# HGRN2 scores of both directions issued together, the last head pair's products moved, weight splits held back

## The chip, the cores and the metric

The kernel runs on one core of a Trainium2 chip. The metric is the device time of one execution in microseconds, median of several. TensorE (PE in the profile) multiplies, VectorE (DVE), ScalarE (ACT) and GpSimd (POOL) work on vectors, SyncE (SP) issues most transfers.

## The reference

Two transformer blocks over 256 tokens of width 1024, all in float32. The first has an HGRN2 mixer over a context of 256 tokens and the 256 latent tokens, in two directions, and a convolutional feed-forward part. The second has retention, sliding-window attention and a second feed-forward part. The change touches the mixer alone:

```python
b = jnp.cumsum(logf, axis=3)
qe = q * jnp.exp(b - b_ref)
ke = k * jnp.exp(b_ref - b)
scores = jnp.where(mask, jnp.einsum('bhnik,bhnjk->bhnij', qe, ke), 0.0)
o_intra = jnp.einsum('bhnij,bhnjv->bhniv', scores, v)
kv = jnp.einsum('bhnjk,bhnjv->bhnkv', k * jnp.exp(b_last - b), v)
...
o_inter = jnp.einsum('bhnik,bhnkv->bhniv', q * jnp.exp(b), s_start)
o = (o_intra + o_inter).reshape(Bn, H, T, v.shape[-1])
...
return (rmsnorm(o, g_gain) * jax.nn.silu(g)) @ w_out
```

There are 8 heads of width 128, chunks of 64 tokens, and for the second direction everything is flipped in time. Only the latent tokens are read out.

## The kernel before

Weights come from HBM in pieces of 512 KB (a half of a chunk) into eight buffers `raw`. Each piece is split in two float32r tiles: `hi` is its rounded copy (ACT, L155), `lo` the rest (DVE, L156). The activations `hT` are split likewise, and a product is three matmuls, weight hi by x hi, hi by lo and lo by hi (`mm3`, L352 to L354). The splits of pieces to come are recorded wherever a chunk is taken or given back (`use`, `part_done`, `release`, all through `pump`), as far ahead as there are free split buffers (five in `split`; more pools come and go). Each engine runs its instructions in the order in which the program records them.

The heads go in four pairs, p = 0 to 3. For each pair there are the products of both forget gates (ff, fb), of q and of v; then gate work on DVE and ACT (`gates`, one generator for each direction d, run step by step together). The attention itself is small float32 work that PE does between the large products. It is queued in `side` and taken out by `tick`, four ticks in a product. For a head hh of the pair it is:

- `T_`: transposes of the decayed context keys `kc`, copied out by ACT to `kcT`
- `SC_`: scores of a direction. 32-column pieces of `ke` against `qe` (L647, L649), the 128x128 block between the two halves of the tokens (L652), and the 64x64 blocks between chunks (L658). They are written to one PSUM bank, masked and copied out by DVE (`copy_predicated`, L664) and ACT; for the second direction DVE adds both into `scm` (L669)
- `S_`: the state from the context (`kcT` by v), `O_`: the output, its squares (ACT) and its norm (POOL and DVE) into `on`
- `OT_`: transposes of `on`, copied to `oTs`

A float32 matmul stands as two passes in the profile, a float32r one as one. For p = 0 to 2 this side work is taken during the next pair's products. For p = 3 it is taken during the four products of g (`C["g", 0..3]`, called G0 to G3 here), by the table `slots`. After each of these, `oTs` of a pair is multiplied by the silu of g (L891) and split into `yh`, `yl` (`split_y`). Then comes the output product `o1` (`row_product`): `go(0)` for the first of its four chunks, and `finish` for the other three, which runs token half 0 first, then `o1_done` on it (DVE L1016 and L1017, ACT), then token half 1, the transposes of the normed rows to `hT` (L978) and the first feed-forward products (L342). `ada_flush` puts the sums of a modulation vector through two matmuls by ones (L599) and adds them (L600).

Of the kernel before, what the change touches and what calls it, by code (L numbers as in the profile page):

```python
# [18 lines left out]
T = 256  # L19
# [32 lines left out]
def kernel(ctx: ExitStack, tc: tile.TileContext, a, out):  # L52
# [42 lines left out]
                   kind)  # L95

    loaded, ready = {}, {}
    at_ = {"l": 0, "s": 0, "u": 0, "rel": 0}
    raw_seq, split_pools = [], []

    class SplitPool:
# [14 lines left out]
    def pump(limit, hold=False):  # L116

        while True:
            go_on = False
            while at_["l"] < len(halves):  # L120
                i = at_["l"]
                parts, k, n, kind = halves[i]
                if kind != "own":
                    o = raw_seq[-RAW_BUFS] if len(raw_seq) >= RAW_BUFS else -1
                    if o >= 0 and not (o < at_["s"] if halves[o][3] == "split" else o < at_["rel"]):
                        break
                    raw_seq.append(i)
                    r = raws.tile([128, 1024], F32, tag="raw", name="raw")
                    rv = r[:, :k * n].rearrange("p (k c) -> p k c", k=k)
                    loaded[i] = (r, rv)  # L130
                else:
                    rv = None
                for f, src in parts:
                    nc.sync.dma_start(f(rv), src)
                at_["l"] += 1
                go_on = True
            i = at_["s"]
            if i < min(len(halves), limit) and i < at_["l"]:
                _, k, n, kind = halves[i]
# [24 lines left out]
            if not go_on:  # L164
                return
# [371 lines left out]
    xr = []  # L537
    for i in range(2):
        t = res.tile([128, D], F32, name=f"x{i}")
        nc.scalar.dma_start(t, a["x"][0][i * 128:(i + 1) * 128, :])  # L540
        xr.append(t)


    yk = hgy.enter_context(tc.tile_pool(name="hgy", bufs=2))
# [72 lines left out]
    def hg_side(p, el, vt):  # L617
# [17 lines left out]
            St[hh] = wk.tile([128, 2, 128], F32, tag="St", name="St")  # L635
            s_.activation(flat(St[hh]), z[:, 0:256], AF.Copy)

        def SC_(hh, d):
            e = el[d]
            z = bank("x")  # L640
            zd = z[:, 0:256].rearrange("p (b t) -> p b t", b=2)
            ha, hb = (0, 32) if d == 0 else (32, 0)
            for b in range(2):
                for c in range(2):
                    o = hh * 256 + b * 128 + 64 * c
                    ra, rb = slice(64 * c + ha, 64 * c + ha + 32), slice(64 * c + hb, 64 * c + hb + 32)
                    t_.matmul(zd[ra, b, 64 * c:64 * c + 64], e["ke"][:, o + ha:o + ha + 32], e["qe"][:, o:o + 64],  # L647
                              start=True, stop=True)
                    t_.matmul(zd[rb, b, rb], e["ke"][:, o + hb:o + hb + 32], e["qe"][:, o + hb:o + hb + 32],  # L649
                              start=True, stop=True)  # L650
            b1, b2 = e["blk"]
            t_.matmul(z[:, 256:384], flat(e["K"][:, hh, b1, e["k"], :]), flat(e["Q"][:, hh, b2, e["c"], :]),  # L652
                      start=True, stop=True)
            rA = slice(0, 64) if d == 0 else slice(64, 128)
            cB = slice(64, 128) if d == 0 else slice(0, 64)
            zo = z[:, 384:512].rearrange("p (b t) -> p b t", b=2)
            for b in range(2):
                t_.matmul(zo[rA, b, :], e["K"][:, hh, b, e["sA"], :], e["Q"][:, hh, b, e["sB"], :],  # L658
                          start=True, stop=True)
            sc = sc_t[d, hh]  # L660
            for c in range(2):
                for r, q_ in ((slice(64 * c, 64 * c + 64), hb), (slice(64 * c + ha, 64 * c + ha + 32), ha)):
                    i = slice(64 * c + q_, 64 * c + q_ + 32)
                    v_.copy_predicated(sc[r, :, i], hmask[r, d:d + 1, i].to_broadcast([r.stop - r.start, 2, 32]),  # L664
                                       zd[r, :, i])
            s_.activation(sc[rA, :, cB], zo[rA], AF.Copy)
            if True and d:
                scm[hh] = wk.tile([128, 2, 128], F32, tag="scm", name="scm", bufs=2)
                v_.tensor_add(scm[hh], sc_t[0, hh], sc)  # L669
            xS[hh, d] = wk.tile([128, 128], F32, tag="xs", name="xs", bufs=4)  # L670
            s_.activation(xS[hh, d], z[:, 256:384], AF.Copy)

        def O_(hh):
            z = bank("x")
            hc = slice(hh * 128, (hh + 1) * 128)
            for b in range(2):
                terms = []
                for d in range(2):
                    e = el[d]
                    b1, b2 = e["blk"]  # L680
                    ql = flat(e["Q"][:, hh, b, e["c"], :]) if b == b1 else e["q2"][:, hh, :]
                    terms.append((ql, St[hh][:, d, :]))
                    if hh in scm:
                        if d:
                            terms.append((scm[hh][:, b, :], vt[:, 2 + b, hc]))
                    else:
                        terms.append((sc_t[d, hh][:, b, :], vt[:, 2 + b, hc]))
                    if b == b2:
                        terms.append((xS[hh, d], vt[:, 2 + b1, hc]))
                for i, (l, r) in enumerate(terms):  # L690
                    t_.matmul(z[:, b * 128:(b + 1) * 128], l, r, start=i == 0, stop=i == len(terms) - 1)  # L691
            ss = small.tile([128, 2], F32, tag="ss2", name="ss2")
            on[hh] = wk.tile([128, 256], F32, tag="on", name="on")
            for b in range(2):
                c = slice(b * 128, (b + 1) * 128)
                s_.activation(on[hh][:, c], z[:, c], AF.Square, accum_out=ss[:, b:b + 1])
# [5 lines left out]
        def OT_(hh):  # L702
            z = bank("x")
            for b in range(2):
                t_.transpose(z[:, b * 128:(b + 1) * 128], on[hh][:, b * 128:(b + 1) * 128], ident)
            s_.activation(oT[p][:, hh, :], z[:, 0:256], AF.Identity, scale=vec("gn"))

        order = [(T_, 0), (T_, 1), (SC_, 0, 0), (SC_, 0, 1), (SC_, 1, 0), (SC_, 1, 1), (S_, 0), (S_, 1),
                 (O_, 0), (O_, 1)]
        late = [(OT_, 0), (OT_, 1)]  # L710
        return tuple([lambda f=f: f[0](*f[1:]) for f in x] for x in (order, late))

# [1 line left out]
    for p in range(4):  # L714
# [59 lines left out]
        def gates(d):  # L774
# [14 lines left out]
            s_.activation(kcv, kcv, AF.Exp)  # L789
            yield  # L790
            v_.tensor_mul(kcv, kcv, kt_[:, 0])

            b = wk.tile([128, 512], F32, tag="b", name="b")
            for hh in range(2):
# [48 lines left out]
            q2 = wk.tile([128, 2, 128], F32, tag="q2", name="q2")  # L843
            for hh in range(2):
                v_.tensor_scalar(q2[:, hh, :], flat(Q[:, hh, b2, cq, :]), EE[:, hh:hh + 1], None, op0=OP.mult)
            el[d] = dict(kc=kcv, qe=qe, ke=ke, Q=Q, K=K, q2=q2, sA=sA, sB=sB, c=cq, k=ck, blk=(b1, b2))
        wv = use(C["v", p])
        gen = [gates(0), gates(1)]
        live = [True, True]
# [1 line left out]
        while any(live):  # L851
# [4 lines left out]
            if nstep in v_steps[p]:  # L856
# [2 lines left out]
                tick(1)  # L859
                if half:  # L860
                    release(C["v", p])
        work, late = hg_side(p, el, vt)
        if p < 3:
            side.extend(work)


    T0, T1, SC00, SC01, SC10, SC11, S0, S1, O0, O1 = work
    OT0, OT1 = late
    slots = [[], [[T0], [T1], [], [SC00]], [[S0], [SC10, S1], [SC01], [SC11]], [[O0], [O1], [], [OT0]]]
    ys = {}  # L870

    def split_y(p):
# [7 lines left out]
    for p in range(4):  # L880
        for x in slots[p]:
            side.append(lambda x=x: [f() for f in x])
        z = fm_product(C["g", p], x=lambda k: hT(k, 256, 512), tag="m", ticks=1)
        drain()
        if p == 2:
            ada_flush()
        if p == 3:
            OT1()
        sg = wk.tile([128, 512], F32, tag="q", name="sg", bufs=2)
        s_.activation(sg, z, AF.Silu)  # L890
        v_.tensor_mul(oTs[:, p, :], oTs[:, p, :], sg)  # L891
        if p:
            split_y(p - 1)
    split_y(3)
    hg.close()
    o1x = ctx.enter_context(ExitStack())
    SplitPool(o1x, "o1split", 6, chunks[C["ug", 1]][1])
# [3 lines left out]
    def row_product(name, n, lhs, done):  # L901
# [7 lines left out]
            mm3(acc[2 * tok + half], lhs(j, kk, tok), (w[kk][0][:, c], w[kk][1][:, c]),  # L909
                j == 0 and kk == 0, j == n - 1 and kk == 1)  # L910

        def go(j):
            if not acc:
                acc.extend(bank("m") for _ in range(4))
            w = use(C[name, j])
            for kk in range(2):
                for tok in range(2):
                    for half in range(2):
                        mms(j, w, kk, tok, half)
                if kk == 0:  # L920
                    part_done(C[name, j])

# [101 lines left out]

    hTh, hTl = h_at(0)
    go, finish = row_product("o1", 4, act_lhs(ys), o1_done)
    for p in range(4 - SKEW):
        go(p)
    f1 = finish(chunks[C["uv", 0]][1])
    nc.scalar.dma_start(vr[:, 1, :], row_bcast(a["b_ada"], 5 * D, D))  # L1030
    gb[5] = vr[:, 1, :]
# [476 lines left out]
```

## Time and profile before

| | |
|---|---|
| median of 3 runs | 875.5 us (874.65 to 876.54) |
| the profiled execution's own time | 873.8 us |
| its span, first to last instruction | 872.0 us |
| PE busy | 856.8 us, 98% of the span |
| PE weight loads | 778.4 us, 89% |
| DVE busy | 599.5 us, 69% |
| ACT busy | 497.8 us, 57% |
| mean granted TensorE clock | 0.997 |

A busy share is an average over the whole span. What limits a stage is seen in that stage, from the rows in order of time and what ended each wait. In the rows below, a matmul's duration includes the fill and the drain of the array, so durations of neighbours overlap; a price on PE is the distance from one start to the next.

### The profile page before, as it was taken

The page shows a single profiled execution, that of the slowest core. Times are in us where ns is not written, and L with a number is a line of the kernel's source. Part 1 is how long each engine was busy: PE and PEld are TensorE (multiplying, and loading weights), DVE is VectorE, ACT ScalarE, POOL GpSimd, SP SyncE. Part 2 cuts the span into 40 slices and gives each one's busy share as a digit, 9 for nine tenths or more (in the row PEclk, how much of TensorE's full clock was granted, in tenths as well). Part 3 has the DMA queues.
Part 4 walks back from the last instruction along what each step waited for, and adds up shares of the span by engine and source line. Part 5 has one row for each costly group of instructions (what it writes and reads, how often), then busy time and mean ns, then how long its engine had stood idle before and what let it go on. Part 6 is the DMA issues. An engine that isn't in the chain of part 4 may idle for free.

```text
span 872.0 us, 15429 instructions
## 1 busy us (share of the span) xinstructions
PE 856.8 (98%) x6216; PEld 778.4 (89%) x6216; DVE 599.5 (69%) x935; ACT 497.8 (57%) x807; POOL 16.3 (2%) x27
## 2 busy tenths in 40 slices
PE   8999999999999999999999999999999999999997
PEld 7688898989978999999998799999999899999995
DVE  5577969776888688977768646765485687555532
ACT  4587474855856666555555646666553675444421
POOL 0000000000000000000000000000000100000000
PEclk9999999999999999999999999999999999999999
DMA  9893653825437368776753574545696097566401
GB/s 355 277 337 109 184 180 125 287 73 170 144 123 240 122 214 272 265 240 203 259 179 85 157 218 119 147 144 165 196 309 201 6 317 247 184 190 190 148 1 49
DMA packets 116360, 161.99 MB, mean 186 GB/s; under 512 B 13888, under 2 KB 95808, under 8 KB 116288
## 3 DMA queue, kind: packets, MB, share of 16 engines
q1 hardware_dynamic: 113984, 155.80, 55.4%
q10 hardware_dynamic: 2304, 5.20, 1.8%
q8 instruction: 49, 0.80, 0.4%
q14 instruction: 23, 0.19, 0.1%
HBM read 159.93 MB, written 1.05 MB: 185 GB/s over the span
## 4 chain that ended last, share of the span: by engine, by line
PE 89%; DVE 5%; ACT 3%; DMA 1%; issue 1%; POOL 0%; SPq 0%; POOLq 0%; DVEq 0%; ACTq 0%
PE m L352 17%; PE m L353 17%; PE m L354 17%; PE x L352 8%; PE x L353 8%; PE x L354 8%; PE x L691 1%; DVE lo L156 1%; PE m L342 1%; PE x L342 1%; PE m L343 1%; PE m L338 1%; PE x L343 1%; PE x L338 1%; DMA raw<-in_f0w_dram 1%
## 5 line engine op out<-in xcount | busy, mean ns | idle before, releaser
L156 DVE TENSOR_TENSOR lo<-raw,hi 128x1024 fp32r<-128x1024 f32 (+1 forms) x248 | 291.1, 1204 | 128.4 <-ACT hi L155 124.5
L155 ACT ACTIVATE hi<-raw 128x1024 fp32r<-128x1024 f32 (+1 forms) x248 | 249.6, 1039 | 115.9 <-PE x L353 47.7
L352 PE MATMUL m<-hT,hi 128*128 128x256 f32 (+1 forms) x560 | 178.2, 318 | 1.4 <-ACT hT L428 1.4
L353 PE MATMUL m<-hT,hi 128*128 128x256 f32 (+1 forms) x560 | 170.5, 304 | 0.5 <-DVE hT L435 0.5
L354 PE MATMUL m<-hT,lo 128*128 128x256 f32 (+1 forms) x560 | 170.8, 305 | 0.1
L352 PE MATMUL x<-hT,hi 128*128 128x256 f32 x592 | 166.5, 281 | 0.0
L353 PE MATMUL x<-hT,hi 128*128 128x256 f32 x592 | 165.9, 280 | 0.0
L354 PE MATMUL x<-hT,lo 128*128 128x256 f32 x592 | 165.9, 280 | 0.0
L352 PEld LDWEIGHTS m<-hT,hi 128*128 128x128 f32 x560 | 105.6, 189 | 12.2 <-issue 5.1
L354 PEld LDWEIGHTS x<-hT,lo 128*128 128x128 f32 x592 | 113.0, 191 | 0.0
L352 PEld LDWEIGHTS x<-hT,hi 128*128 128x128 f32 x592 | 111.4, 188 | 1.0 <-ACT hi L155 0.2
L353 PEld LDWEIGHTS x<-hT,hi 128*128 128x128 f32 x592 | 111.1, 188 | 1.0 <-issue 0.2
L353 PEld LDWEIGHTS m<-hT,hi 128*128 128x128 f32 x560 | 105.7, 189 | 5.9 <-DVE hT L435 1.1
L354 PEld LDWEIGHTS m<-hT,lo 128*128 128x128 f32 x560 | 105.4, 188 | 5.8 <-DVE lo L156 0.3
L352 PE MATMUL m<-hi,ah 128*128 128x512 f32 x248 | 96.7, 390 | 0.0
L354 PE MATMUL m<-hi,al 128*128 128x512 f32 x248 | 96.6, 390 | 0.0
L353 PE MATMUL m<-lo,ah 128*128 128x512 f32 x248 | 96.6, 389 | 0.0
L354 PEld LDWEIGHTS m<-hi,al 128*128 128x128 f32 x248 | 46.6, 188 | 9.8 <-DVE al L1149 0.2
L353 PEld LDWEIGHTS m<-lo,ah 128*128 128x128 f32 x248 | 46.6, 188 | 8.8
L352 PEld LDWEIGHTS m<-hi,ah 128*128 128x128 f32 x248 | 46.5, 188 | 8.7
L582 DVE SCALAR_TENSOR_TENSOR vr<-raw,cs,vr 128x1024 f32<-128x1024 f32 x28 | 35.9, 1281 | 0.4
L352 PE MATMUL m<-hi,hT 128*128 128x256 f32 x128 | 35.8, 280 | 0.0
(302 smaller groups left out, 1250.7 us busy)
## 6 DMA issues: line engine op xcount, KB each, us to landing
raw<-in_ffn_w_up_dram SPq DMA_DIRECT2D x44, 512.0 KB, 5.6
raw<-in_w_in_dram SPq DMA_DIRECT2D x42, 512.0 KB, 4.1
raw<-in_hg_w_in_dram SPq DMA_DIRECT2D x36, 512.0 KB, 5.0
raw<-in_w_ada_dram SPq DMA_DIRECT2D x32, 512.0 KB, 5.0
raw<-in_w_up_dram SPq DMA_DIRECT2D x32, 512.0 KB, 4.7
raw<-in_w_down_dram SPq DMA_DIRECT2D x32, 512.0 KB, 3.7
raw<-in_ffn_w_down_dram SPq DMA_DIRECT2D x22, 512.0 KB, 4.3
raw<-in_ada_dram SPq DMA_DIRECT2D x16, 512.0 KB, 6.2
```

What stands on the lines that cost most here:

```text
L155: s_.activation(h[:, :w], r[:, :w], AF.Copy)
L156: held.append(lambda r=r, h=h, l=l, w=w: v_.tensor_tensor(l[:, :w], r[:, :w], h[:, :w].bitcast(F32), op=OP.subtract))
L338: t_.matmul(o, hTl[:, k, c], w[k][0], start=False, stop=k == KT - 1)
L342: t_.matmul(o, hTh[:, k, c], w[k][0], start=k == 0, stop=False)
L343: t_.matmul(o, hTh[:, k, c], w[k][1], start=False, stop=False)
L352: t_.matmul(o, wh, xh, start=start, stop=False)
L353: t_.matmul(o, wh, xl, start=False, stop=False)
L354: t_.matmul(o, wl, xh, start=False, stop=stop)
L582: v_.scalar_tensor_tensor(acc, w[kk][0], cs[:, k:k + 1], acc, op0=OP.mult, op1=OP.add)
L691: t_.matmul(z[:, b * 128:(b + 1) * 128], l, r, start=i == 0, stop=i == len(terms) - 1)
```

## The change

1. `SC_` now does both directions of a head in one call: first the two 128x128 matmuls, then all 32-column matmuls of both directions, dealt round the four groups of 32 output partitions. The 64x64 blocks are cut into two 32-column matmuls each. The masks and copies of both directions follow. A place in the queue that it frees is filled with a call that does nothing.
2. For p = 3, G0 is recorded inside the gate loop, right behind the second half of v, with `T_` of both heads in its last two ticks. `S_` goes into G1, the first scores to the end of G2, the second scores and `O_` into G3, `OT_` into `go(0)` of the output product.
3. The table `at_["cap"]` holds back the splits of weights: none of `o1` before the second scores, one piece more at `go(0)`, the rest behind the last `split_y`. `ada_flush` moves there too.
4. The last pair's `on` and its silu of g live in the second half of `x`, whose load moves from the start of the mixer to behind these splits (on the ACT queue).

```diff
-            if i < min(len(halves), limit) and i < at_["l"]:
+            if i < min(len(halves), limit, at_["cap"]) and i < at_["l"]:
...
-        nc.scalar.dma_start(t, a["x"][0][i * 128:(i + 1) * 128, :])
+    nc.scalar.dma_start(xr[0], a["x"][0][0:128, :])
...
-        def SC_(hh, d):
+        def SC_(hh):
...
+            zs, groups = [], [[] for _ in range(4)]
+            for d in range(2):
+                e = el[d]
+                z = bank("x")
+                zs.append(z)
+                b1, b2 = e["blk"]
+                t_.matmul(z[:, 256:384], flat(e["K"][:, hh, b1, e["k"], :]), flat(e["Q"][:, hh, b2, e["c"], :]),
+                          start=True, stop=True)
...
+                for b in range(2):
+                    for i in range(2):
+                        g = 2 * d + i
+                        groups[g].append((zo[32 * g:32 * g + 32, b, :], e["K"][:, hh, b, e["sA"], 32 * i:32 * i + 32],
+                                          e["Q"][:, hh, b, e["sB"], :]))
+                    for c in range(2):
+                        o = hh * 256 + b * 128 + 64 * c
+                        ga, gb_ = 2 * c + ha // 32, 2 * c + hb // 32
+                        rb = slice(32 * gb_, 32 * gb_ + 32)
+                        groups[ga].append((zd[32 * ga:32 * ga + 32, b, 64 * c:64 * c + 64],
+                                           e["ke"][:, o + ha:o + ha + 32], e["qe"][:, o:o + 64]))
+                        groups[gb_].append((zd[rb, b, rb], e["ke"][:, o + hb:o + hb + 32],
+                                            e["qe"][:, o + hb:o + hb + 32]))
+            for n in range(max(len(g) for g in groups)):
+                for g in groups:
+                    if n < len(g):
+                        t_.matmul(*g[n], start=True, stop=True)
...
-        order = [(T_, 0), (T_, 1), (SC_, 0, 0), (SC_, 0, 1), (SC_, 1, 0), (SC_, 1, 1), (S_, 0), (S_, 1),
-                 (O_, 0), (O_, 1)]
+        order = [(T_, 0), (T_, 1), (SC_, 0), (len, ()), (SC_, 1), (len, ()), (S_, 0), (S_, 1), (O_, 0), (O_, 1)]
...
+                    if p == 3:
+
+                        side.extend([lambda: None] * 2 + work[0:2])
+                        zg = fm_product(C["g", 0], x=lambda k: hT(k, 256, 512), tag="m", ticks=1)
...
-    slots = [[], [[T0], [T1], [], [SC00]], [[S0], [SC10, S1], [SC01], [SC11]], [[O0], [O1], [], [OT0]]]
+    slots = [[], [[S0], [S1], [], []], [[], [], [], [SC0]],
+             [[SC1, lambda: splits_to(o1_at[0] + 1)], [], [O0], [O1]]]
...
-    for p in range(4 - SKEW):
-        go(p)
+    at_["cap"] = o1_at[1]
+    side.extend([lambda: None, OT0, lambda: None, OT1])
+    go(0, 1)
+    drain()
+    v_.tensor_mul(oTs[:, 3, :], oTs[:, 3, :], sg)
+    split_y(3)
+    ada_flush()
+    splits_to(1 << 30)
+    nc.scalar.dma_start(xr[1], a["x"][0][128:256, :])
```

First place: PE, the scores of one head of the pairs p = 0 to 2 (the same in all of them; `x` is the PSUM bank). Before, with the line of dots for three more pairs of such rows:

```order
L647 MATMUL x<-qe,ke 32x64
L649 MATMUL x<-qe,ke 32x32
...
L652 MATMUL x<-Q,K 128x128
L658 MATMUL x<-Q,K 64x64 x2
L647 MATMUL x<-qe,ke 32x64
L649 MATMUL x<-qe,ke 32x32
```

The changed kernel, its 24 narrow matmuls cut to the first rows:

```order
L648 MATMUL x<-Q,K 128x128 x2
L669 MATMUL x<-Q,K 32x64 x2
L669 MATMUL x<-qe,ke 32x64
L669 MATMUL x<-qe,ke 32x32
L669 MATMUL x<-qe,ke 32x64
...
L669 MATMUL x<-Q,K 32x64 x4
```

The narrow, the 128-wide and the 64-wide matmuls of one direction were followed by those of the other; now the 128-wide ones of both stand together, then only narrow ones.

Second place: DVE, from the end of the last pair's gate work on (L156 is the rest of a weight split). Before:

```order
L669 TENSOR_TENSOR scm<-sct_621,sct_625 128x256
L600 TENSOR_TENSOR vr<-vr,x 128x512 x2
...
L699 TENSOR_SCALAR on<-x,r 128x128 x2
L156 TENSOR_TENSOR lo<-raw,hi 128x1024
L891 TENSOR_TENSOR oTs<-oTs,sg 128x512
L877 TENSOR_TENSOR yl<-oTs,yh 128x512 x2
L156 TENSOR_TENSOR lo<-raw,hi 128x1024 x9
L1016 TENSOR_TENSOR oTs<-m,vr 128x512
```

The changed kernel at the same place:

```order
L686 TENSOR_TENSOR scm<-sct_620,sct_624 128x256
L156 TENSOR_TENSOR lo<-raw,hi 128x1024 x3
...
L1054 TENSOR_TENSOR oTs<-oTs,x_606 128x512
L903 TENSOR_TENSOR yl<-oTs,yh 128x512
L600 TENSOR_TENSOR vr<-vr,x 128x512 x2
L156 TENSOR_TENSOR lo<-raw,hi 128x1024 x9
L1039 TENSOR_TENSOR oTs<-m,vr 128x512
```

Three splits stand in one piece behind the second scores, nine still stand between the last `yl` and the first instruction of `o1_done`, and the two additions of `ada_flush` are now ahead of those nine.

## Rows read from the trace of the kernel before

**Rows 1.** The page: busy time by engine; the chain that ended last, by engine.

```profile
PE 856.8 (98%) x6216; PEld 778.4 (89%) x6216; DVE 599.5 (69%) x935; ACT 497.8 (57%) x807; POOL 16.3 (2%) x27
...
PE 89%; DVE 5%; ACT 3%; DMA 1%; issue 1%; POOL 0%; SPq 0%; POOLq 0%; DVEq 0%; ACTq 0%
```

**Rows 2.** Timeline, PE, a head's scores in p = 1: start us, us, instruction.

```profile
87.86 0.40 PE L354 MATMUL m<-hT,lo 128*128 128x512 f32 x1
88.19 0.24 PE L647 MATMUL x<-qe,ke 128*32 128x64 f32 x1
...
88.34 0.27 PE L647 MATMUL x<-qe,ke 128*32 128x64 f32 x3
88.54 0.49 PE L652 MATMUL x<-Q,K 128*128 128x128 f32 x2
88.96 0.45 PE L658 MATMUL x<-Q,K 128*64 128x64 f32 x4
...
90.48 0.50 PE L352 MATMUL m<-hT,hi 128*128 128x512 f32 x1
90.82 0.40 PE L353 MATMUL m<-hT,hi 128*128 128x512 f32 x1
```

**Rows 3.** The chain in order of time: start us, us, what; prices of PE work.

```profile
24.37 1.00 PE x L403 x16
...
84.62 0.87 PE x L625 x8
...
98.77 1.78 PE x L633 x16
...
101.97 1.78 PE x L691 x16
```

**Rows 4.** Timeline, DVE: the last step of direction 1 that scores need.

```profile
88.77 0.42 DVE L836 TENSOR_TENSOR K<-K,b 128x256 f32<-128x256 f32 x1
```

**Rows 5.** The same step one pair later.

```profile
138.93 0.42 DVE L836 TENSOR_TENSOR K<-K,b 128x256 f32<-128x256 f32 x1
```

**Rows 6.** Timeline, PE, the matmul ahead of the scores there.

```profile
139.93 0.40 PE L354 MATMUL m<-hT,lo 128*128 128x512 f32 x1
```

**Rows 7.** Timeline, PE, last pair: waits in brackets, with what ended them.

```profile
241.60 1.16 PE L633 MATMUL x<-vt,kcT 128*128 128x128 f32 x8 [1.38 <-ACT kcT L627]
...
264.56 0.59 PE L705 MATMUL x<-ident,on 128*128 128x128 f32 x2 [0.51 <-DVE on L699]
```

**Rows 8.** Timeline, PE: G0, G1, L599, `go(0)`, `finish`, the transposes of `o1_done`.

```profile
225.04 0.36 PE L352 MATMUL m<-hT,hi 128*128 128x256 f32 x1
...
230.78 0.28 PE L352 MATMUL m<-hT,hi 128*128 128x256 f32 x1
...
252.07 1.98 PE L599 MATMUL x<-vr,ones 128*128 128x512 f32 x4
...
264.90 0.48 PE L352 MATMUL m<-hi,yh 128*128 128x512 f32 x1
...
270.46 0.39 PE L352 MATMUL m<-hi,yh 128*128 128x512 f32 x1
...
285.43 1.04 PE L978 MATMUL x<-ident,oTs 128*128 128x128 f32 x8
```

**Rows 9.** Timeline, DVE: `ada_flush`, last splits, `o1_done`.

```profile
258.01 1.28 DVE L600 TENSOR_TENSOR vr<-vr,x 128x512 f32<-128x512 f32 x2
...
266.79 1.48 DVE L877 TENSOR_TENSOR yl<-oTs,yh 128x512 fp32r<-128x512 f32 x2
268.52 10.31 DVE L156 TENSOR_TENSOR lo<-raw,hi 128x1024 fp32r<-128x1024 f32 x9 [0.26 <-ACT hi L155]
278.75 0.68 DVE L1016 TENSOR_TENSOR oTs<-m,vr 128x512 f32<-128x512 f32 x1
```

**Rows 10.** Timeline, ACT: the end of `o1_done` for token half 0.

```profile
283.21 0.73 ACT L1004 ACTIVATE oTs<-x,r 128x512 f32<-128x512 f32 x1 [0.97 <-POOL r L319]
```

**Rows 11.** DMA issues by line: size, median us from issue to landing.

```profile
x<-in_x_dram ACTq DMA_DIRECT2D x2, 512.0 KB, 7.1
```

More of the change, by code (lines that the diff above doesn't have):

```diff
@@ L97 @@
     loaded, ready = {}, {}
-    at_ = {"l": 0, "s": 0, "u": 0, "rel": 0}
+    at_ = {"l": 0, "s": 0, "u": 0, "rel": 0, "cap": 1 << 30}
     raw_seq, split_pools = [], []
@@ L636, in S_ @@
             s_.activation(flat(St[hh]), z[:, 0:256], AF.Copy)
-        def SC_(hh, d):
[L639 to L643, printed above, removed]
-                for c in range(2):
[L645 to L671, printed above, removed]
@@ new lines, in SC_ @@
+        def SC_(hh):
[7 more added lines that the diff above has]
+                          start=True, stop=True)
+                zd = z[:, 0:256].rearrange("p (b t) -> p b t", b=2)
+                zo = z[:, 384:512].rearrange("p (b t) -> p b t", b=2)
+                ha, hb = (0, 32) if d == 0 else (32, 0)
+                for b in range(2):
[15 more added lines that the diff above has]
+                        t_.matmul(*g[n], start=True, stop=True)
+            for d in range(2):
+                z, sc = zs[d], sc_t[d, hh]
+                zd = z[:, 0:256].rearrange("p (b t) -> p b t", b=2)
+                zo = z[:, 384:512].rearrange("p (b t) -> p b t", b=2)
+                ha, hb = (0, 32) if d == 0 else (32, 0)
+                rA = slice(0, 64) if d == 0 else slice(64, 128)
+                cB = slice(64, 128) if d == 0 else slice(0, 64)
+                for c in range(2):
+                    for r, q_ in ((slice(64 * c, 64 * c + 64), hb), (slice(64 * c + ha, 64 * c + ha + 32), ha)):
+                        i = slice(64 * c + q_, 64 * c + q_ + 32)
+                        v_.copy_predicated(sc[r, :, i], hmask[r, d:d + 1, i].to_broadcast([r.stop - r.start, 2, 32]),
+                                           zd[r, :, i])
+                s_.activation(sc[rA, :, cB], zo[rA], AF.Copy)
+                xS[hh, d] = wk.tile([128, 128], F32, tag="xs", name="xs", bufs=4)
+                s_.activation(xS[hh, d], z[:, 256:384], AF.Copy)
+            scm[hh] = wk.tile([128, 2, 128], F32, tag="scm", name="scm", bufs=2)
+            v_.tensor_add(scm[hh], sc_t[0, hh], sc_t[1, hh])
@@ L682, in O_ @@
                     terms.append((ql, St[hh][:, d, :]))
[L683 to L687, printed above, removed]
+                    if d:
+                        terms.append((scm[hh][:, b, :], vt[:, 2 + b, hc]))
                     if b == b2:
@@ L692, in O_ @@
             ss = small.tile([128, 2], F32, tag="ss2", name="ss2")
-            on[hh] = wk.tile([128, 256], F32, tag="on", name="on")
+            on[hh] = wk.tile([128, 256], F32, tag="on", name="on") if p < 3 else xr[1][:, hh * T:hh * T + T]
             for b in range(2):
@@ L791, in gates @@
             v_.tensor_mul(kcv, kcv, kt_[:, 0])
+            el[d] = dict(kc=kcv)
             b = wk.tile([128, 512], F32, tag="b", name="b")
@@ L845, in gates @@
                 v_.tensor_scalar(q2[:, hh, :], flat(Q[:, hh, b2, cq, :]), EE[:, hh:hh + 1], None, op0=OP.mult)
-            el[d] = dict(kc=kcv, qe=qe, ke=ke, Q=Q, K=K, q2=q2, sA=sA, sB=sB, c=cq, k=ck, blk=(b1, b2))
+            el[d].update(qe=qe, ke=ke, Q=Q, K=K, q2=q2, sA=sA, sB=sB, c=cq, k=ck, blk=(b1, b2))
+        work, late = hg_side(p, el, vt)
         wv = use(C["v", p])
@@ L861, with splits_to @@
                     release(C["v", p])
-        work, late = hg_side(p, el, vt)
+                    if p == 3:
+                        side.extend([lambda: None] * 2 + work[0:2])
+                        zg = fm_product(C["g", 0], x=lambda k: hT(k, 256, 512), tag="m", ticks=1)
         if p < 3:
             side.extend(work)
-    T0, T1, SC00, SC01, SC10, SC11, S0, S1, O0, O1 = work
+    _, _, SC0, _, SC1, _, S0, S1, O0, O1 = work
+    def splits_to(i):
+        at_["cap"] = i
+        pump(len(halves))
+    at_["cap"] = chunks[C["g", 3]][1]
     OT0, OT1 = late
-    slots = [[], [[T0], [T1], [], [SC00]], [[S0], [SC10, S1], [SC01], [SC11]], [[O0], [O1], [], [OT0]]]
+    o1_at = [chunks[C["o1", j]][1] for j in range(4)]
+    slots = [[], [[S0], [S1], [], []], [[], [], [], [SC0]],
+             [[SC1, lambda: splits_to(o1_at[0] + 1)], [], [O0], [O1]]]
     ys = {}
@@ L882 @@
             side.append(lambda x=x: [f() for f in x])
-        z = fm_product(C["g", p], x=lambda k: hT(k, 256, 512), tag="m", ticks=1)
+        z = fm_product(C["g", p], x=lambda k: hT(k, 256, 512), tag="m", ticks=1) if p else zg
         drain()
[L885 to L889, printed above, removed]
+        sg = wk.tile([128, 512], F32, tag="q", name="sg", bufs=2) if p < 3 else xr[1][:, 512:1024]
         s_.activation(sg, z, AF.Silu)
-        v_.tensor_mul(oTs[:, p, :], oTs[:, p, :], sg)
+        if p < 3:
+            v_.tensor_mul(oTs[:, p, :], oTs[:, p, :], sg)
         if p:
             split_y(p - 1)
-    split_y(3)
     hg.close()
@@ L910, in mms, with go @@
                 j == 0 and kk == 0, j == n - 1 and kk == 1)
-        def go(j):
+        def go(j, ticks=0):
             if not acc:
@@ L919, in go @@
                         mms(j, w, kk, tok, half)
+                    tick(ticks)
                 if kk == 0:
```

## Prediction

> **What bounds the kernel now.** I read the page first. PE is busy for 98% of the span, and the chain that ended last runs on PE for 89% of it [rows 1]. So nearly everything else is paced by PE, and a microsecond of PE work removed in a stage where nothing else comes last is a microsecond of the whole. Then I read PE's timeline through the mixer. In the first three pairs PE stands still nowhere; in the last pair there are waits, the two longest 1.38 and 0.51 us [rows 7], because the gate work on DVE and ACT and the small steps between PE, ACT and DVE have no later pair to hide under. A third reading, DVE's timeline behind the last pair, shows a queue of nine splits that ends at 268.52 + 10.31 = 278.83, just where `o1_done` begins (278.75) [rows 9].
>
> **The scores on PE.** One head's scores lie between the matmul at 87.86 and the one at 90.82, 2.96 us [rows 2]. A 512-column float32r step takes (270.46 - 264.90)/24 = 0.232 us [rows 8], and two such steps would lie there anyway, so the scores cost 2.96 - 0.46 = 2.50 us.
>
> What is in it: per direction 0.35 us from the first narrow matmul to the 128-wide ones, 0.42 from there to the 64-wide ones, and the rest, to half of 90.48 - 88.19, 0.37 [rows 2]. A pass of 128 columns takes 0.11 (16 of L633 in 1.78 [rows 3]), so I price one of 64 columns at 0.055 and one of 32 at 0.03. The eight narrow matmuls are 16 passes, which all start by about 88.4 [rows 2]: they overlap in their four groups of 32 output partitions, and a group has four of them, 0.22 at most. The two 128-wide passes are 0.22, the four 64-wide ones 0.22 in one group. That is 1.3 us of passes for both directions; the other 1.2 us of the 2.50 go with the seven changes of width (128 to 32, 128, 64, 32, 128, 64, 128), 0.17 each.
>
> After: four 128-wide passes, 0.44, with no change ahead of them. Then 24 narrow matmuls, each group with four of 64 columns and two of 32, in two passes each: 8 x 0.055 + 4 x 0.03 = 0.56. Two changes: 0.34. Together 1.34, so 1.16 saved per head. The four-group overlap holds for longer rows too: 16 passes of 256 columns in 1.00 us (L403) [rows 3], 0.25 for each of four in a group.
>
> The unknown is the 48 narrow passes in a row, over two PSUM banks, which no row shows. Bounds: 0.56 us if the groups overlap in full, 48 x 0.05 = 2.4 if not at all. I take 0.56, since 16 passes in the same dealing round did so.
>
> The Trainium skill speaks against it: "TensorE: Matmul & The Clock Gate", Part 1, gives a floor of about 25 ns between the starts of matmuls, however short they are. By it 48 passes take 1.2 us, and a head would save 0.5 instead of 1.16. The rows contradict it: 16 starts within 0.2 us are some 13 ns each [rows 2].
>
> **A wait that comes in.** The second 128-wide matmul needs direction 1's gates at once; before, they were needed 1.15 us later. In the first pair their last step ends at 88.77 + 0.42 = 89.19 [rows 4], and PE would be there at 87.86 + 0.23 + 0.22 = 88.31: a wait of 0.93 us with the latency. Behind it in PE's queue stand the narrow matmuls and the rest of the product, so it is paid in full. One pair later the step ends at 139.35 [rows 5] and PE arrives at 139.93 + 0.45 = 140.38 [rows 6]: 1.0 us spare, and this spare stays, since gates and PE both start from the q product. So in the pairs p = 1 to 3 (scores of 0 to 2): 6 x 1.16 - 0.93 = 6.0 us. DVE and ACT have the masks and copies of before, in the same order. The weight splits there start when PE gives a buffer back, so they move with PE, and PE waits for none of them now.
>
> **The last pair.** I count from G0's start, 225.04, which moves with all that is ahead of it. PE until G3's end: four products at 5.7 (230.78 - 225.04) [rows 8], `T_` 0.87, `S_` 1.78, `O_` 2 x 1.78 [rows 3], scores 2 x 1.34: 31.7, so 256.7. `T_` is at three quarters of G0, where `kc` is just ready; the gates slip by 1.15 us, a third split (10.31/9 [rows 9]) now being ahead of them on DVE, but the scores stand a whole product later than before. So the 1.38 wait should go. `go(0)` takes 5.56, both `OT_` 0.5: the second ends at 262.8, against 264.90 before [rows 8]. L599's two matmuls are moved, not saved.
>
> Behind the second `OT_` comes a DVE chain as long as before. Before, 264.90 to 278.83: 13.9 us. After: ACT's copy, the product by silu, the split on ACT and DVE, both L600 (1.28, moved here), nine `lo` (10.31) [rows 9], 14.2 in all, since one `yl` (0.74) is already done and so is the silu. `o1_done` can start at 277.0; it took 283.94 - 278.75 = 5.2 us to the normed rows [rows 9, 10], so 282.2. PE's own work is there earlier: 262.8 + 1.9 (L599) + 14.97 (270.46 to 285.43) [rows 8] = 279.7. PE waits 2.5 us there, and the transposes come at 282.2 in place of 285.43: 3.2 us gained, not the 5.7 that PE alone would give. The load of `x` is issued on ACT behind eight splits of about 1.1 us (as on DVE), near 273, and lands 7.1 us later [rows 11], about 280; its first use is behind the 282.2.
>
> **Sum.** 6.0 + 3.2 = 9.2 us. The profiled execution's own time is 873.8 (span 872.0), so it would be 864.6; the median of the runs is 1.7 higher, and there it is 875.5 - 9.2 = **866.3**.
>
> **Rivals.**
> - *The passes are issued no faster than in the row.* If the 0.35 us from 88.19 to 88.54 is an issue rate for 16 passes (22 ns each) and not the time of a group, 48 passes take 1.05. A head saves 0.67; over eight heads 3.9 us are missing: 870.2. For it: no longer run of them is shown. Against: four L658 passes alone take 0.37, sixteen narrow ones 0.35 [rows 2], so the price goes by group and not by count. By the floor of the Trainium skill cited above it would be about 871.
> - *The last pair gives nothing.* The held-back splits reach DVE no earlier, because a link ahead (the `on` of the second head, at `OT_`) slips by 2 us or a split is missed in the second chunk: 6.0 remain, 869.5.
> - *The last pair gives all of PE's 5.7,* if DVE's chain is shorter than I count: 863.8.
> - *Slower.* The dealing over two banks makes the groups take turns: 48 passes at 0.05 are 2.4 us, and a head costs 3.17 in place of the 1.34 that I count. Over eight heads that is 14.6 us, against 9.2 gained: 875.5 + 5.4 = 881. It decides at 0.56 + 9.2/8 = 1.7 us for the 48 passes, 36 ns each.
>
> **How the numbers follow.** Forecast (864.3 to 868.3) 0.55, issue rate 0.13, last pair nothing 0.12, last pair in full 0.12, slower 0.04, and 0.04 for a small net change of both signs. The range from 863 to 871.5 takes in the forecast, both neighbours above and the one below, about 0.85 when their own spread is taken off. 0.2% (1.75 us) is about what a measurement here can tell from no change. Faster: 0.92; same 0.04; slower 0.04.
>
> **What would show it.** In PE's timeline of a head in p = 2 or 3, from the last large matmul to the second one behind the scores: 1.8 us in place of 2.96, with the narrow passes starting within 0.6 us. A wait of about 0.9 us at L648 in the first pair alone. In the last pair no wait at L633, the second `OT_` 2 us earlier against G0 than before, DVE's nine splits running into L1039 without a pause, and a wait of 2 to 3 us at the transposes L1001. It is wrong if the narrow passes take 1 us or more, if PE waits for splits in `finish`, or if weights in the first three pairs come late.

## The result and the profile after

The changed kernel takes 865.75 us (median of 4 runs, 864.85 to 868.15) where the kernel before takes 875.08 beside it (874.08 to 876.54): a ratio of 0.9896, 95% interval 0.9872 to 0.9921. A second measurement, the control below, gave 0.9898 (0.9882 to 0.9915). The profiled execution took 864.85 us, its span is 863.0.

The page, busy time by engine and the chain that ended last:

```profile
PE 847.1 (98%) x6280; PEld 772.6 (90%) x6280; DVE 599.3 (69%) x935; ACT 497.0 (58%) x807; POOL 16.3 (2%) x27
...
PE 89%; DVE 5%; ACT 4%; issue 1%; DMA 0%; POOL 0%; POOLq 0%; DVEq 0%; ACTq 0%
```

PE is 9.7 us less busy with 64 more passes (32 matmuls); DVE and ACT do what they did [rows 1]. PE's timeline in the first pair's first head (a wait in brackets), and then in the second pair's first head:

```profile
87.35 0.39 PE L354 MATMUL m<-hT,lo 128*128 128x512 f32 x1
87.58 0.38 PE L648 MATMUL x<-Q,K 128*128 128x128 f32 x2
88.74 0.49 PE L648 MATMUL x<-Q,K 128*128 128x128 f32 x2 [0.78 <-DVE K L848]
89.16 0.25 PE L669 MATMUL x<-Q,K 128*32 128x64 f32 x2
...
138.18 0.40 PE L354 MATMUL m<-hT,lo 128*128 128x512 f32 x1
138.41 0.61 PE L648 MATMUL x<-Q,K 128*128 128x128 f32 x4
138.95 0.25 PE L669 MATMUL x<-Q,K 128*32 128x64 f32 x2
...
139.45 0.29 PE L669 MATMUL x<-qe,ke 128*32 128x32 f32 x9
139.67 0.50 PE L352 MATMUL m<-hT,hi 128*128 128x512 f32 x1
140.01 0.39 PE L353 MATMUL m<-hT,hi 128*128 128x512 f32 x1
```

From the last large matmul to the second one behind the scores it is 140.01 - 138.18 = 1.83 us, against 2.96 before [rows 2]. From the first narrow matmul to the next product it is 0.72, with one change of width in it. In the first pair the second L648 matmul comes 1.16 us behind the first, where two such passes take 0.22: 0.94 us of waiting for DVE's L848.

PE in the last pair, from the second `OT_` (L717) to the transposes of the normed rows (L1001) and the first feed-forward product (L342):

```profile
256.38 0.38 PE L717 MATMUL x<-ident,x 128*128 128x128 f32 x2
256.60 0.59 PE L599 MATMUL x<-vr,ones 128*128 128x512 f32 x1
...
261.77 0.50 PE L353 MATMUL m<-lo,yh 128*128 128x512 f32 x1 [0.34 <-DVE lo L156]
...
273.69 0.39 PE L354 MATMUL m<-hi,yl 128*128 128x512 f32 x1
275.82 1.06 PE L1001 MATMUL x<-ident,oTs 128*128 128x128 f32 x8 [1.74 <-DVE oTs L1026]
...
278.84 0.39 PE L342 MATMUL x<-hi,hT 128*128 128x256 f32 x1 [0.56 <-DVE hT L1019]
```

And DVE over the same stretch:

```profile
257.30 0.69 DVE L1054 TENSOR_TENSOR oTs<-oTs,x 128x512 f32<-128x512 f32 x1 [0.59 <-ACT oTs L718]
258.69 0.69 DVE L903 TENSOR_TENSOR yl<-oTs,yh 128x512 fp32r<-128x512 f32 x1 [0.70 <-ACT yh L902]
259.30 1.28 DVE L600 TENSOR_TENSOR vr<-vr,x 128x512 f32<-128x512 f32 x2
260.50 10.30 DVE L156 TENSOR_TENSOR lo<-raw,hi 128x1024 fp32r<-128x1024 f32 x9
270.72 0.68 DVE L1039 TENSOR_TENSOR oTs<-m,vr 128x512 f32<-128x512 f32 x1
...
275.59 0.68 DVE L1039 TENSOR_TENSOR ep<-m,vr 128x512 f32<-128x512 f32 x1
276.31 0.69 DVE L1040 TENSOR_TENSOR x<-x,ep 128x512 f32<-128x512 f32 x1
276.92 0.68 DVE L1016 TENSOR_TENSOR hf<-x,AB 128x512 f32<-128x512 f32 x1
```

The nine splits [rows 9] still run into `o1_done` without a pause. The transposes come at 275.82 in place of 285.43 [rows 8]. In the output product PE waits once for one of these splits, 0.34 us at 261.77.

**Where the time went**, by starts on PE of the first matmul of a step. From `T_` of the first pair to `T_` of the third: 104.15 before, 100.63 after, 3.52 less. From there to the transposes L1001: 96.83 and 91.25, 5.58 less. From these to the transposes of the second token half 0.44 are lost again (8.36 and 8.80), and 0.20 in the rest. That is 8.46; the other 0.5 of the 8.95 between the two own times lies ahead of the first `T_`, in code that both kernels share but for one load. It is not the change's for sure: in the twelve runs below that first `T_` comes between 83.7 and 88.0 us, and in each trace the clock falls to its lower level (1.2 GHz) for some us within the first 30. So kernels are compared below from one place of the program to another.

### The profile page after: what moved, and what is told of

The parts are those of the page before. It is cut to its first block, busy times and chain, and to the rows that moved or that the text cites. A ratio compares the mean times of both kernels' runs of the same rounds, so it can differ in the third digit from the quotient of the medians.

```text
span 863.0 us, 15556 instructions
## 1 busy us (share of the span) xinstructions
PE 847.1 (98%) x6280; PEld 772.6 (90%) x6280; DVE 599.3 (69%) x935; ACT 497.0 (58%) x807; POOL 16.3 (2%) x27
## 3 DMA queue, kind: packets, MB, share of 16 engines
HBM read 159.93 MB, written 1.05 MB: 187 GB/s over the span
## 4 chain that ended last, share of the span: by engine, by line
PE 89%; DVE 5%; ACT 4%; issue 1%; DMA 0%; POOL 0%; POOLq 0%; DVEq 0%; ACTq 0%
PE m L352 17%; PE m L354 16%; PE m L353 16%; PE x L352 8%; PE x L353 8%; PE x L354 8%; PE x L703 2%; ACT hi L155 1%; PE x L342 1%; PE m L342 1%; PE m L343 1%; PE m L338 1%; PE x L343 1%; PE x L633 1%; PE x L338 1%
## 5 line engine op out<-in xcount | busy, mean ns | idle before, releaser
L156 DVE TENSOR_TENSOR lo<-raw,hi 128x1024 fp32r<-128x1024 f32 (+1 forms) x248 | 291.0, 1204 | 122.8 <-ACT hi L155 119.6
L582 DVE SCALAR_TENSOR_TENSOR vr<-raw,cs,vr 128x1024 f32<-128x1024 f32 x28 | 35.9, 1281 | 0.4
```

Source lines behind the costliest of these rows:

```text
L156: held.append(lambda r=r, h=h, l=l, w=w: v_.tensor_tensor(l[:, :w], r[:, :w], h[:, :w].bitcast(F32), op=OP.subtract))
L582: v_.scalar_tensor_tensor(acc, w[kk][0], cs[:, k:k + 1], acc, op0=OP.mult, op1=OP.add)
```

## Experiments

### What the scores cost: two orders of the narrow matmuls, and one more change of width

**By group.** A column group's six matmuls behind one another:

```diff
-            for n in range(max(len(g) for g in groups)):
-                for g in groups:
-                    if n < len(g):
-                        t_.matmul(*g[n], start=True, stop=True)
+            for g in groups:
+                for m in g:
+                    t_.matmul(*m, start=True, stop=True)
```

> The changed kernel with one edit: the 24 narrow matmuls of a head are issued one column group after the other, six matmuls each, instead of dealt out in turn. Theory (the overlap comes of four groups standing next to each other in PE's queue): 48 passes take about 0.05 us each, 2.4 us, a head 1.8 us more, the kernel about 14 us more, 880. Rival (passes of different groups overlap whatever their order, or the price goes by count): no change, 865.8.

876.0 us, ratio 1.0011 (0.9994 to 1.0027): all that the change gains is gone. PE's timeline of the same head:

```profile
145.54 0.30 PE L668 MATMUL x<-Q,K 128*32 128x64 f32 x2
...
147.31 0.28 PE L668 MATMUL x<-qe,ke 128*32 128x64 f32 x2
147.51 0.50 PE L352 MATMUL m<-hT,hi 128*128 128x512 f32 x1
```

147.51 - 145.54 = 1.97 in place of 0.72. The order decides, as the theory had it; the size was 10 us, not 14, because a pass costs 38 ns here and not 50: 1.97 less about 0.15 for the change of width at its end (an estimate; the prediction has 0.17 for one), divided by 48. Within a group the starts stand 0.056 apart for 64 columns, and where one group follows another they overlap.

**Two groups at a time.**

```diff
-            for n in range(max(len(g) for g in groups)):
-                for g in groups:
+            for two in (groups[0:2], groups[2:4]):
+                for n in range(max(len(g) for g in two)):
+                    for g in two:
```

> The changed kernel with one edit: the 24 narrow matmuls of a head are dealt out over two column groups at a time, 12 matmuls each, instead of over all four. Theory (passes of different groups overlap, so the price of a pass is that of one group, 38 ns measured, divided by the groups that take turns): 48 passes at 19 ns are 0.9 us, a head 0.35 more, the kernel plus 2.8 us. Rival (only the weight load of the next pass has to find another group, so that two groups are enough): no change.

869.2 us, ratio 0.9931 (0.9913 to 0.9949), 2.9 us over the changed kernel beside it by the two ratios, 2.5 by the medians. The same head:

```profile
140.00 0.31 PE L670 MATMUL x<-Q,K 128*32 128x64 f32 x4
...
140.99 0.28 PE L670 MATMUL x<-qe,ke 128*32 128x64 f32 x4
141.19 0.50 PE L352 MATMUL m<-hT,hi 128*128 128x512 f32 x1
```

1.19 us from the first narrow matmul to the product. Less the same 0.15, a pass costs 38, 22 and 12 ns on average with one, two and four groups taking turns: not far from one over the number of groups (19 and 9.5). The expected 0.9 us and 2.8 us were 1.04 and 2.9.

**The wide ones in the middle.** The four 128-wide passes stand behind the third round of narrow ones:

```diff
-                t_.matmul(z[:, 256:384], flat(e["K"][:, hh, b1, e["k"], :]), flat(e["Q"][:, hh, b2, e["c"], :]),
-                          start=True, stop=True)
+                wide.append((z[:, 256:384], flat(e["K"][:, hh, b1, e["k"], :]), flat(e["Q"][:, hh, b2, e["c"], :])))
...
             for n in range(max(len(g) for g in groups)):
+                for m in wide if n == 3 else ():
+                    t_.matmul(*m, start=True, stop=True)
```

> The changed kernel with one edit: the two 128-wide score matmuls of a head stand in the middle of the narrow ones, behind their third round, instead of ahead of them. Theory (a change of tile width costs 0.17 us): two more changes, 0.34 us, and about 0.1 of passes that no longer overlap at the seam: a head takes 2.3 instead of 1.83 us; the first pair's wait moves to the first narrow matmul and keeps 0.6 to 1.0 us. Eight heads: plus 2.7 to 3.6 us, about 869. Rival (a change of width costs nothing by itself, and the narrow passes alone were dear): 865.8 or less.

869.0 us, ratio 0.9918 (0.9894 to 0.9942). A head of the second pair:

```profile
140.42 0.40 PE L354 MATMUL m<-hT,lo 128*128 128x512 f32 x1
...
142.66 0.40 PE L353 MATMUL m<-hT,hi 128*128 128x512 f32 x1
```

It takes 2.24 us in place of 1.83, 0.41 for two changes of width and the seam in the dealing together. That fits the expected 0.34 and 0.1; a change of width by itself no run isolates, so 0.17 stays an estimate.

### The two halves of the change apart

**The scores alone**, the last pair as before:

```diff
-            if i < min(len(halves), limit, at_["cap"]) and i < at_["l"]:
+            if i < min(len(halves), limit) and i < at_["l"]:
...
-    slots = [[], [[S0], [S1], [], []], [[], [], [], [SC0]],
-             [[SC1, lambda: splits_to(o1_at[0] + 1)], [], [O0], [O1]]]
+    slots = [[], [[T0], [T1], [], []], [[S0], [S1], [SC0], [SC1]], [[O0], [O1], [], [OT0]]]
```

> The kernel before with one edit: both directions' scores of a head together; the last pair's products stay where they were before. Theory (scores give 5.8 us in the first three pairs, and in the last pair two thirds of the gain come from the moved products and held-back splits): the first-pair wait of 0.9 us is there, the last pair's wait at the scaling splits stays as before, the last pair gives 0 to 2.5, the time is 867 to 869.5 where the kernel before has 875.1. Rival (the merged scores explain everything, the last pair's new order nothing): 865.8.

868.5 us, ratio 0.9914 (0.9894 to 0.9935). From the third pair's `T_` to the transposes it takes 93.11: 3.72 less than before, 2.28 of it the third pair's scores, so 1.44 in the last pair. PE there:

```profile
234.26 0.28 PE L354 MATMUL m<-hT,lo 128*128 128x256 f32 x1
237.07 1.21 PE L633 MATMUL x<-vt,kcT 128*128 128x128 f32 x8 [2.52 <-ACT kcT L627]
```

And by windows: its bounds and length, busy time of PE, weight loads, DVE, ACT, POOL with counts, granted clock, DMA share, GB/s:

```profile
236.00:238.00 2.00, 0.93 (x9) 0.93 (x9) 1.96 (x7) 2.00 (x4) 0.00 (x0) 1.00 0.00 0
238.00:240.00 2.00, 2.00 (x11) 1.81 (x10) 2.00 (x3) 1.75 (x4) 0.00 (x0) 0.51 0.33 53
240.00:242.00 2.00, 2.00 (x15) 2.00 (x13) 2.00 (x4) 1.03 (x2) 0.00 (x0) 0.64 0.74 234
```

With the old places PE comes to `S_` earlier and waits 2.52 us for the gates in place of 1.38 [rows 7]; behind it the clock is at its lower level for three us, 2 x 0.49 + 2 x 0.36 = 1.7 us of PE's work. So part of what shorter scores save in the last pair is waited away. In the changed kernel, with `T_` and `S_` moved, there is no wait at L633 and the granted clock stays at 1.00.

**The moves alone**, the scores one direction at a time as before:

```diff
-        def SC_(hh):
+        def SC_(hh, d):
...
-    slots = [[], [[S0], [S1], [], []], [[], [], [], [SC0]],
-             [[SC1, lambda: splits_to(o1_at[0] + 1)], [], [O0], [O1]]]
+    slots = [[], [[S0], [S1], [], []], [[], [], [], [SC00, SC01]],
+             [[SC10, SC11, lambda: splits_to(o1_at[0] + 1)], [], [O0], [O1]]]
```

> The changed kernel with one edit: each direction's scores again by themselves, in the order and with the tile widths of before; the last pair's new places and the held-back splits stay. Theory: no wait in the first pair and nothing gained in the first three; in the last pair the scores cost 2.3 us more than in the changed kernel, so the second output transpose comes only about 0.3 us or less ahead of its old place against the first G product, and the gain is 0 to 1.5 us: 873.6 to 875. Rival (the new order alone is worth the last pair's 3.2): 872 or less.

875.1 us, ratio 0.9995 (0.9981 to 1.001). The transposes come 1.31 us earlier after the third pair's `T_` than before; 0.45 of it are lost behind them, as in the changed kernel. The rest is too small for the timing. The rival (872 or less) falls. Scores and moves together give 3.3 in the last pair, where apart they give 1.44 and 1.31.

### The wait in the first pair

`S_` ahead of the scores, in the first pair alone:

```diff
+        if p == 0:
+            order[2:8] = order[6:8] + order[2:6]
```

> The changed kernel with one edit: in the first pair alone the state products stand ahead of the scores in the side queue, so that the scores come one place later. Theory (the first pair's wait of 0.94 us at the second 128-wide matmul is for direction 1's gates alone): the wait goes, no new one comes (the transposed kc is copied 2 us before the state products), minus 0.9 us, 864.9. Rival (something else behind the scores is late by then, or ACT's copy of kc is): no change, 865.8.

868.4 us, ratio 0.9914 (0.9886 to 0.9943): the forecast gain didn't come, and the interval overlaps the changed kernel's, so the timing alone doesn't show a loss. The trace does: the wait at the second L648 is gone (1.83 us a head), but from the first pair's `T_` to the second's it takes 52.21 in place of 50.84. PE behind the first pair's outputs:

```profile
107.77 0.28 PE L354 MATMUL m<-hT,lo 128*128 128x256 f32 x1
108.50 2.18 PE L605 MATMUL x<-ones,vr 128*128 128x2 f32 x16 [0.46 <-DVE vr L582]
```

And its windows (PE alone):

```profile
104.00:108.00 4.00, 4.00 (x35) 1.00 0.99 311
108.00:112.00 4.00, 3.54 (x24) 0.75 0.91 285
112.00:116.00 4.00, 4.00 (x31) 0.82 1.06 364
```

The second head's masks start on DVE at 98.52 (96.53 in the changed kernel), so the last modulation sums (L582) behind them end at 108.36 (106.36). The two-column matmuls L605 wait for these, and then the clock falls: 4 x 0.25 + 4 x 0.18 = 1.7 us. In the changed kernel the same sixteen matmuls run without a wait in front of them, and these windows have a clock of 1.00. The theory counted what waits for the scores and left out what stands behind them in DVE's queue.

### The queue of nine splits

**Three of them later**, one behind the first half's normed rows and two behind its transposes:

```diff
+            if at_["cap"] < 1 << 30:
+                at_["cap"] = 1 << 30
+                pump(len(halves), True)
             f0 = [next(d0) for _ in range(4)][-1]
+            if held:
+                held.pop(0)()
...
-    splits_to(1 << 30)
+    splits_to(o1_at[3] + 2)
```

> The changed kernel with one edit: of the nine DVE splits behind the last y, the last three (weights of the feed-forward block, first used 13 us later) are held back: one is put behind the first token half's normed rows, two behind its transposes. Theory (the wait of 1.9 us at the transposes comes from DVE's nine splits, 10.3 us): DVE starts the first half's rows 3.4 us earlier, PE's products are then the later ones, the wait at the transposes goes, a shorter one of up to 0.5 us comes at the second half's transposes; minus 1.2 to 1.9 us, about 864.3. Rival (the wait comes from another link, or the splits put off are missed by the feed-forward products): 865.8 or more.

866.15 us, ratio 0.9885 (0.9859 to 0.9912): not told apart from 0.9896. The waits of PE over 0.2 us in the stage (us in total, times, longest):

```profile
PE x L1006 <- DVE ep L1031: 1.6, 1, 1.6
PE x L1101 <- ACT oTs L1093: 0.4, 1, 0.4
PE m L353 <- DVE lo L156: 0.3, 1, 0.3
PE x L342 <- DVE hT L1024: 0.2, 1, 0.2
```

The wait at the first transposes is gone; they come 89.37 us after the third pair's `T_` in place of 91.25. So the nine splits made it. But 1.40 come back at the second half's transposes, where DVE now has two splits ahead of that half's rows, and 0.5 up to the second block (and 0.67 there, which the combined run below doesn't show).

**None held back:** `cap` takes no part.

```diff
-        at_["cap"] = i
...
-    at_["cap"] = chunks[C["g", 3]][1]
...
-    at_["cap"] = o1_at[1]
```

> The changed kernel with one edit: no split is held back; the output's and the feed-forward block's weights are split as early as buffers allow, eight of the nine now ahead of the last product by silu on DVE. Theory (the splits' sum on DVE sets the stage's end, wherever they stand): the wait moves from the transposes to the fourth product's first y, about 2.4 us there, the transposes come within 1 us of the changed kernel's: 865 to 866.8. Rival (holding the splits back is what brings the last pair's 3.2 us): 868 or more.

867.3 us, ratio 0.9897 (0.9873 to 0.9922), the changed kernel's own; the median lies between the theory's 866.8 and the rival's 868. That the whole hardly changes was as expected, the place of the wait was not:

```profile
251.17 0.39 PE L703 MATMUL x<-St,q 128*128 128x128 f32 x2
253.69 0.49 PE L703 MATMUL x<-vt,scm 128*128 128x128 f32 x2 [2.14 <-DVE scm L686]
```

A split ahead of the second head's masks on DVE makes `O_` wait 2.1 us, and the clock falls behind it (0.50 from 256 to 258). The transposes come 1.51 later than in the changed kernel (92.76 and 91.25), more than the 1 us expected, and 0.7 of that is won back behind them; the first pair took 0.5 less in that execution, a shorter wait at L648 that has nothing to do with the edit. So the holding back is worth about 0.8 us in this trace, which the timing can't show.

**Both edits and a gap.** The first-pair order, the three late splits, and `ada_flush` ahead of `split_y(3)`:

```diff
+    ada_flush()
     split_y(3)
-    ada_flush()
```

> The changed kernel with the edits of the two runs above that put off three splits and that reorder the first pair, and with DVE's two additions of the ada rows ahead of the last y's split, in a gap of 0.7 us. Theory: minus 1.2 to 1.9, minus 0.9, and 0.4 off the wait inside the output product: 862.6 to 863.3. Rival (the two waits hide one another or something behind them): 864.5 or more.

865.7 us, ratio 0.9875 (0.9849 to 0.9901): the lowest, but not apart from the changed kernel. It misses the theory's 862.6 to 863.3. Its transposes come at 88.71, 2.5 earlier; 1.3 and 0.5 come back as above, and the first pair loses 1.5.

**Two splits on GpSimd**, with the changed kernel beside it on the same chip:

> The changed kernel itself, as a control on the chip of the three runs beside it: 0.9896 of the kernel before, as first measured; a difference under 0.2% between it and the others is not told apart.

The control: 866.7 us, ratio 0.9898, and stage by stage the same times (91.25 from the third pair's `T_` to the transposes).

```diff
-                    held.append(lambda r=r, h=h, l=l, w=w: v_.tensor_tensor(
+                    eng = nc.gpsimd if i in on_pool else v_
+                    held.append(lambda r=r, h=h, l=l, w=w, eng=eng: eng.tensor_tensor(
...
+    on_pool.update(range(o1_at[3] + 2, o1_at[3] + 4))
     splits_to(1 << 30)
```

> The changed kernel with one edit: of the nine splits behind the last y, the two of the feed-forward block's first weights (first used 13 us later) are subtracted on GpSimd instead of DVE. Theory (in this stretch it is DVE's sum of work that counts, so putting splits off gives back later what it gains, and only taking them off DVE keeps it): the first half's rows start 2.3 us earlier, the wait at the transposes (1.9) and most of that behind them (0.6) go and nothing comes back at the second half: minus 1.9 to 2.4 us against the control, if a GpSimd split takes under 3.3 us; above that it delays the rows' power step on GpSimd. Rival (the stretch is bounded by another link, or GpSimd and DVE get in each other's way): within 0.5 us of the control or slower.

869.4 us, ratio 0.9926 (0.9909 to 0.9943), against 0.9898 for the control: 2.5 us slower. DVE and POOL:

```profile
261.20 12.44 DVE L158 TENSOR_TENSOR lo<-raw,hi 128x1024 fp32r<-128x1024 f32 x7
266.88 3.43 DVE L158 TENSOR_TENSOR lo<-raw,hi 128x1024 fp32r<-128x1024 f32 x1
...
270.24 3.41 DVE L158 TENSOR_TENSOR lo<-raw,hi 128x1024 fp32r<-128x1024 f32 x1
...
266.08 3.14 POOL L158 TENSOR_TENSOR lo<-raw,hi 128x1024 fp32r<-128x1024 f32 x1 [11.04 <-ACT hi L156]
...
269.19 3.38 POOL L158 TENSOR_TENSOR lo<-raw,hi 128x1024 fp32r<-128x1024 f32 x1
```

The first row is all seven of DVE's splits; the next two are its last two by themselves. While POOL does its two (3.1 and 3.4 us), DVE's take 3.4 where one takes 1.22 alone, and each ends 1.1 us behind the end of POOL's, at 270.31 and 273.65 after 269.22 and 272.57, as if it had run only then. Between DVE's ends POOL has 2.3 us for each of its own (270.31 to 272.57 for the second), so the rest of its 3.1 and 3.4 is waiting for DVE, by this estimate. Seven take 12.44, nine took 10.30. PE then waits 3.9 us at the transposes and the clock falls behind that (0.50 from 278 to 284). The rival holds: the two engines block one another. The Trainium skill says so: "SBUF — State Buffer", Who interferes with whom, has a VectorE instruction with two SBUF inputs contend with a GpSimd one that reads SBUF, for a shared port that only one of them holds at a time. The ends above agree.

> The run with two splits on GpSimd, and with DVE's two additions of the ada rows ahead of the last y's split, in a gap of 0.7 us. Theory: 0.4 us more than that run gains (the wait inside the output product): minus 2.3 to 2.8 us against the control. Rival: no difference from that run.

With `ada_flush` ahead of `split_y(3)` as well (the edit above): 868.1 us, 0.9911 (0.9892 to 0.9929). The wait inside the output product is gone, and that at the transposes is 3.0 in place of 3.9; the clock stayed up here. The gain over the control that was forecast isn't there; the medians differ by 0.16%, which is not told apart. In the trace the transposes come 91.89 us after the third pair's `T_`, 0.64 later than in the control. DVE beside POOL's second split here, which runs until 274.45:

```profile
272.11 0.68 DVE L1041 TENSOR_TENSOR oTs<-m,vr 128x512 f32<-128x512 f32 x1
272.82 2.17 DVE L1042 TENSOR_TENSOR x<-x,oTs 128x512 f32<-128x512 f32 x1
```

L1041, which reads one operand from PSUM (`m`), takes its usual 0.68; L1042, with both in SBUF, takes 2.17 where it takes 0.69 alone. So it is VectorE work with two SBUF operands that GpSimd held up.

## Why the prediction was right

Forecast 866.3 with 864.3 to 868.3 as the likeliest case; measured 865.75. The interval of the ratio is 2.1 us to either side, so that the two medians are only 0.6 apart is in part luck; what bears the forecast out is its terms, read from the trace.

- *A head's scores:* 1.80 forecast, 1.83 measured. The 0.56 us for the 48 narrow passes was the unknown. By group they take 38 ns each, dealt over two groups 22, over four 12, so the price goes by group, as assumed, and two more changes of width cost 0.41 with the seam, which fits 0.17 each. The issue-rate rival (1.05 us for the 48 passes) falls: they take 0.57. The floor of 25 ns between starts that the Trainium skill gives in "TensorE: Matmul & The Clock Gate", Part 1, does not hold for these passes in four column groups; 12 ns were measured. Counted by whole float32 matmuls of two passes it is 24 ns, so a floor for each of those is not excluded here. The rival that the groups take turns falls too; 1.82 us in the by-group order shows what that costs: no gain.
- *The wait in the first pair:* 0.93 forecast, 0.94 in the profiled execution, whose first head took 1.04 us over the others' 1.83. The wait was as long in three more traces (the control, the first GpSimd run and the by-group run), but 0.35 in five with the same order there: PE's arrival against DVE's gates differs between executions. What sets it is open.
- *First three pairs:* 6.0 forecast. 3.52 from the first `T_` to the third pair's and 2.3 of the third pair's scores make 5.8.
- *Last pair:* 3.2 forecast, 3.3 measured (5.58 less 2.3). No wait at L633; the second `OT_` is 2.0 us earlier against G0 than before (2.1 forecast); counted from G0's start, now 218.74, `o1_done` was forecast at 270.7 and began at 270.72. The wait at the transposes was 1.9 by starts (2.13 less a step of 0.23), not 2.5, as PE came 0.5 later than forecast: 0.49 by starts are the wait for a split at 261.77. The prediction had named a wait for splits in `finish` as a sign of being wrong; it came once, ahead of a place where PE waits for DVE anyway. That DVE's nine splits make the wait at the transposes is shown: with three of them later it is gone.
- *What was missed:* 0.44 us behind the transposes. DVE's L1039 and L1040 of the second half now stand ahead of L1016 when the transposes come, so L342 waits 0.56. This 0.44 is the larger part of what the sum of 9.2 has too much against the 8.46 above, and by luck the 0.5 ahead of the first `T_` hides that in the own times (8.95).
- *Shown beyond the prediction:* the 3.3 of the last pair is not the moves' gain. The moves alone give 1.31, the scores alone 1.44; together 0.55 more than the sum. That the moves take away the wait at L633 and the fall of the clock that cost the scores alone 1.7 us is in the traces; whether that is all of it was not tested.

## What to carry to other kernels

Small matmuls that fill a quarter of the array's columns should be dealt out over the four column groups, and all of one width put together: the order alone was worth 10 us here, a change of width about 0.17 by estimate. When a queue of vector work sets a stage's end, moving its pieces behind the first consumer only moves the wait to the second; look at the sum of the engine's work up to the last one, and don't hand pieces to GpSimd beside VectorE without a trial. A wait of PE's can cost more than its length, if the clock falls behind it.

## What was not expected of the hardware

- The clock fell to its lower level behind a wait of 2.5 us and one of 2.1, and behind one of 3.9 in one run, but not behind 3.0 in another, and not behind the changed kernel's 1.7. It also fell behind waits of 0.46 and 0.52 (the combined run) followed by sixteen two-column matmuls. By the granted clock a fall cost 1.7 us in four of these five runs, and 3.4 in the one behind 3.9. What decides whether it falls is open.
- A float32 split of 128x1024 took 3.1 to 3.5 us on GpSimd beside VectorE's (about 2.3 of its own, by the estimate above) where VectorE needs 1.2, and VectorE's own is stretched to 3.4 meanwhile.
- Executions of kernels that share their start reach the first `T_` up to 4 us apart, more than most edits here are worth.
